# A two-block network on one core: the down factors kept as plain fp32 and split in the down stage, and all block sums on VectorE

## The chip, the core and the metric

The kernel runs on one core of one Trainium2 chip. The number that counts is the device time of one execution in microseconds (us). The engines of a core are named as the profile names them: PE is TensorE (PEld its weight loads), DVE is VectorE, ACT is ScalarE, POOL is GpSimd, and SP is SyncE, which here only issues DMAs. Every engine works through its own queue in the order in which the instructions stand in it; an instruction that has to wait holds up all that stand behind it on that engine.

## What is computed

Two transformer-like blocks run one after the other on 1024 tokens of width 1024. The change lies in their two feed-forward networks, which are alike in size (hidden width 2816):

```python
# first block
gu = jnp.einsum('bsd,df->bsf', x, w_gu)
gate, up = gu[..., :FFN_HIDDEN], gu[..., FFN_HIDDEN:]
ffn = jnp.einsum('bsf,fd->bsd', jax.nn.silu(gate) * up, w_down)
return layer_norm(DEEPNORM_ALPHA * x + ffn, ln2_g, ln2_b)
...
# second block
f = (jax.nn.silu(h @ w_gate[l]) * (h @ w_up[l])) @ w_down[l]
x = x + gate_f * rmsnorm(f, g_ffn_post[l])
```

All products are made in fp32 accuracy. The kernel splits each fp32 factor in a high part (a cast on ACT to the rounded type that PE takes) and a low part (the difference, on DVE or POOL) and makes three matmuls of them: high by high, high by low, low by high.

## The kernel before

**Stages.** The first feed-forward network (FFN1, tiles x1...) takes its gate and up products from about 751 us to 1226 us and its down stage until about 1405 us; the second (FFN2, tiles x3...) from about 2065 us to 2496 us and until about 2672 us. Before them, in between and after them lie the attention, mixing and output projections, which the change does not touch.

**Gate and up.** The hidden units go in pairs of blocks of 128. The first two pairs are made directly (`direct`), the other nine by a seven-product scheme for a 2x2 block matrix (class `Matrix`, Strassen-Winograd). A pair needs one `Gate` and one `Up` matrix of seven products each, a product being 12 matmuls of 128x512. For each product a weight factor is split into a tile `wst` (cast on ACT at L945; low part at L946, on POOL for products 2 and 4, else on DVE). Some weight factors are sums of blocks first (tile `tt`, L925, DVE). The results leave PSUM by DVE adds (tiles `u` and `p`, L963 to L976) and by ACT. The other factors of the seven products are blocks of the activations and sums of them: T1, T2, T3, T4, made once in `SAct.sums` (L838). Before, T1 and T4 are made on POOL, T2 and T3 on DVE; T4 is written into the tile of block B12 when the direct products have read that for the last time.

**The factors of the down stage.** The hidden activations of a pair are turned into seven left factors for the down products (`forms`, L1034: A11, A22, A12 and the sums S1 to S4, which write over a11, a12, a21 and s1 in place) and stored in DRAM (`store`, L1026). Before, `store` takes a slot "w", splits the factor in it (tile `hf`: cast on ACT, low part on DVE, L80 and L84) and stores both parts, 512 KB. A store is issued on ACT's queue only when the next one comes (`flush`). The slots "w" are six, and `wst` takes its tiles from the same six. In FFN1 a side task also runs through this stage: `cond_steps` multiplies rows of w_cond (`raw_c`, 512 KB a load) into `mod` on DVE.

**Down.** `down` (L1129) goes over the pairs in groups of 1, 2, 2, 2 and 2, with seven products in each. The left factors of a product lie in one of the seven tiles of the activations (`act.next`, a ring), to which DMAs bring both parts from DRAM. The right factors are blocks of w_down or sums of them (`st`), split into `ws` (ACT and DVE). PE goes through the products; each result is added to an accumulator by DVE (`dacc` and `acc`, L1196). After the groups `down_last` adds four hidden blocks that were kept as they are (`hl_d`).

**Order.** The program is recorded in source order, and a scheduler then sets each engine's order; work under `soon()` gets a high priority in it.

```python
SLOTS = {"raw": 3, "w": 6}
def slot(tag, shape, dtype, name):
    return strm.tile(shape, dtype, tag=tag, bufs=SLOTS[tag], name=name)
```

Of the kernel before, what the change touches and what calls it, by code (L numbers as in the profile page):

```python
# [9 lines left out]
F32 = mybir.dt.float32  # L10
F32R = mybir.dt.float32r
# [10 lines left out]
S = 1024  # L22
D = 1024
P = 128
# [14 lines left out]
def two_blocks(ctx: ExitStack, tc: tile.TileContext, a):  # L39
# [16 lines left out]
    def slot(tag, shape, dtype, name):  # L56
        return strm.tile(shape, dtype, tag=tag, bufs=SLOTS[tag], name=name)
# [16 lines left out]
    def soon():  # L74
        return tc.high_priority(offset=4000)
# [132 lines left out]
    for h, l, k0, nk in wu0:  # L208
        for j in range(nk):
            k = k0 + j  # L210
# [566 lines left out]
    class SAct:  # L777
# [4 lines left out]
        def __init__(self, name):  # L782
            self.name = name
            self.high, self.high_done = pool(f"{name}b")
            hi = [self.high.tile([P, 4, 512], F32R, name=f"{name}{n}")
                  for n in ("B11h", "B11l", "B21h", "B21l", "B12l", "B22h", "B22l")]
            self.t = {"B11": hi[0:2], "B21": hi[2:4], "B22": hi[5:7]}

            self.ring, self.n = hi, 0

        def second_half(self):

# [3 lines left out]
            self.t["T4"] = self.t["B12"]  # L796

        def next(self):
            self.n += 1
            return self.ring[(self.n - 1) % len(self.ring)]  # L800

        def __call__(self, n):
            if n not in self.t:
# [34 lines left out]
        def sums(self):  # L838
            def sub(n, ts, eng, x, y):

                t = self.temp()
                (xh, xl), (yh, yl) = ([b.bitcast(F32)[:, :, ts] for b in self(z)] for z in (x, y))
                eng.tensor_tensor(t, xh, yh, op=OP.subtract)
                eng.tensor_tensor(t, t, xl, op=OP.add)
                eng.tensor_tensor(t, t, yl, op=OP.subtract)
                self.part(n, ts, t, eng)
                return t

            chunks = [slice(c * P, (c + 1) * P) for c in range(4)]
            for ts in chunks:  # L850
                t1 = sub("T1", ts, G, "B12", "B11")
                sub("T3", ts, V, "B22", "B12")
                t = self.temp()
                xh, xl = (b.bitcast(F32)[:, :, ts] for b in self("B22"))
                V.tensor_tensor(t, xh, t1, op=OP.subtract)
                V.tensor_tensor(t, t, xl, op=OP.add)
                self.part("T2", ts, t, V)
            for ts in chunks:
                sub("T4", ts, G, "B21", "T2")

    def norm_stats(x):

# [37 lines left out]
    NLAST, SIZES = 4, (1, 2, 2, 2, 2)  # L900
    NPAIR = (NFT - NLAST) // 2
    FORMS = ("A11", "S3", "S2", "A22", "S1", "A12", "S4")
    h_d = [{n: dr.tile([P, 2, 512], F32, name=f"h_d{i}{n}") for n in FORMS} for i in range(NPAIR)]
    hl_d = [dr.tile([P, 2, S], F32, name=f"hl_d{i}") for i in range(NLAST)]

    class Matrix:

# [88 lines left out]
    class Ffn:  # L996
# [29 lines left out]
        def store(self, dst, x):  # L1026

            self.flush()
            t = slot("w", [P, 2, 512], F32R, "hf")
            with soon():  # L1030
                split(t[:, 0], t[:, 1], x)
            self.stores.append((dst, t.bitcast(F32)))

        def forms(self, i, b):  # L1034


            if i >= NPAIR:
                plain = lambda j, th: self.store(hl_d[2 * (i - NPAIR) + j][:, :, th * 512:(th + 1) * 512], b[j, th])
                for n in ((0, 0), None, (1, 1), (1, 0), None, (0, 1)):
                    if n:  # L1040
                        plain(*n)
                    yield
                return
            put = lambda n, x: self.store(h_d[i][n], x)
            put("A11", b[0, 0])
            yield
            yield
            put("A22", b[1, 1])
            yield
            put("A12", b[1, 0])  # L1050
            yield
            yield
            a11, a12, a21, a22 = b[0, 0], b[1, 0], b[0, 1], b[1, 1]
            s1 = self.post("s1")
            V.tensor_tensor(s1, a21, a22, op=OP.add)
            V.tensor_tensor(a21, a11, a21, op=OP.subtract)
            put("S3", a21)
            yield
            V.tensor_tensor(a11, s1, a11, op=OP.subtract)
            put("S2", a11)  # L1060
            yield
            put("S1", s1)
            yield
            V.tensor_tensor(a12, a12, a11, op=OP.subtract)
            put("S4", a12)
            yield
# [62 lines left out]
        def down(self, wd, res=None):  # L1129
# [24 lines left out]
            for g, np_ in enumerate(SIZES):  # L1154
# [18 lines left out]
                a = [ps_lg(), ps_lg()]  # L1173
                for m, (p, ln, rn) in enumerate(((1, "A11", "B11"), (7, "S3", "T3"), (6, "S2", "T2"), (4, "A22", "T4"),
                                                 (5, "S1", "T1"), (2, "A12", "B21"), (3, "S4", "B22"))):
                    hs, ws = act.next(), []
                    for j in range(np_):
                        DMA.dma_start(hs.bitcast(F32)[:, 2 * j:2 * j + 2, :], h_d[f + j][ln])
                        w = slot("w", [P, 2, 512], F32R, "ws")
                        with soon():  # L1180
                            split(w[:, 0], w[:, 1], block(rn, j))
                        ws.append(w)
                    if p in (7, 2):
                        b = [ps_mm(512), ps_mm(512), *(ps_tr().rearrange("p a b -> p (a b)") for _ in range(2))]
# [1 line left out]
                    for c0, n in ((0, 2), (2, 2)) if p in (1, 6, 5, 3) else ((c, 1) for c in range(4)):  # L1186
                        o = a[c0 // 2] if n == 2 else b[c0][:, None, :]
                        for i in range(n):
                            ts = slice((c0 + i) * P, (c0 + i + 1) * P)
                            for j in range(np_):  # L1190
                                mm3(o[:, i, :], hs[:, 2 * j, ts], hs[:, 2 * j + 1, ts], ws[j][:, 0], ws[j][:, 1],
                                    not more and j == 0, j == np_ - 1, more)
                        x = acc_of(p, c0, n)
                        with soon():
                            if g > 0:
                                V.tensor_tensor(x, x, o, op=OP.add)  # L1196
                            elif res is not None and p not in own:
                                V.scalar_tensor_tensor(x, x, ALPHA, o, op0=OP.mult, op1=OP.add)
                            else:
                                A.copy(x, o)  # L1200
                        q = {4: 6, 2: 1}.get(p)
                        if lastg and q:
                            V.tensor_tensor(x, x, acc_of(q, c0, n), op=OP.add)
                        elif lastg and p == 5:
                            x7 = acc_of(7, c0, n)
                            V.tensor_tensor(x7, x7, x, op=OP.add)
# [5 lines left out]
            halves = lambda t: [flat(t)[:, i * S:(i + 1) * S] for i in range(2)]  # L1212
            self.hs, self.ws = [], []
            for n in range(NLAST):
                t = act.next()
                DMA.dma_start(flat(t).bitcast(F32), hl_d[n].rearrange("p a b -> p (a b)"))
                self.hs.append(halves(t))
            for n in range(NLAST):
                t = halves(act.next()) if n else [slot("w", [P, S], F32R, "last") for _ in range(2)]
                split(*t, nxt[n])  # L1220
                self.ws.append(t)
            for done in (dp_done, self.pp_done, self.gp_done):
# [428 lines left out]
    n = 0  # L1651
# [121 lines left out]
```

## Time and profile before

| what | value |
|---|---|
| time, median of 3 runs (lowest, highest) | 2727.97 us (2725.17, 2728.15) |
| profiled execution: its time, its span | 2729.37 us, 2727.6 us |
| busy PE, DVE, ACT, POOL | 89%, 67%, 40%, 29% of the span |
| mean granted PE clock | 0.945 |
| feed-forward gate and up, FFN1 and FFN2 | 475 us and 431 us |
| down groups and last blocks' start, FFN1 and FFN2 | 179 us and 176 us |

The span runs from the first to the last instruction; 1.8 us of the execution lie around it. The four stages of the last two lines are 1261 us, 46% of the span. Busy shares over the whole span mix stages with different limits, so what a change does is read in its own stages: how many matmuls a stage holds, how long it takes, and what PE waited for in it.

### The profile page before, as it was taken

The numbers are of one execution on the slowest core, as the hardware profiler recorded it, in microseconds if no ns is written. First come the engines' busy times: TensorE is split into PE (matmuls) and PEld (weight loads), VectorE is DVE, ScalarE is ACT, GpSimd is POOL, SyncE is SP. The second block draws the span as 40 slices with busy tenths as digits, with TensorE's granted clock in tenths as the row PEclk, the third lists the DMA queues.
The fourth block names the chain that finished last, engine by engine and source line by source line (L and its number), as shares of the span: only waits on it lengthen the run. The fifth ranks groups of instructions, "written<-read, shape, count | busy, mean of one in ns | idle before, by whom it ended". The sixth has DMA issues, their size and how long they took to land.

```text
span 2727.6 us, 32854 instructions
## 1 busy us (share of the span) xinstructions
PE 2419.6 (89%) x11584; PEld 1977.9 (73%) x11584; DVE 1840.7 (67%) x3042; ACT 1099.3 (40%) x2013; POOL 784.8 (29%) x751
## 2 busy tenths in 40 slices
PE   8889997998988887889997989898888898999998
PEld 8868775886766665668876868677666666777886
DVE  4889789457667777758776366767555656556775
ACT  4559864243233222323226344445733323334221
POOL 2510235037422122120026042527552212122004
PEclk9999997999998998999998999999989999899999
DMA  4153546333435554567732434553414323337763
GB/s 175 59 153 113 147 137 178 83 98 105 162 127 190 178 179 158 179 249 252 261 141 108 129 105 132 175 159 100 164 58 151 139 108 125 114 124 254 252 226 124
DMA packets 171724, 414.00 MB, mean 152 GB/s; under 512 B 21788, under 2 KB 67868, under 8 KB 170536
## 3 DMA queue, kind: packets, MB, share of 16 engines
q1 hardware_dynamic: 149064, 337.45, 38.2%
q10 hardware_dynamic: 22496, 74.46, 6.8%
q8 instruction: 92, 1.51, 0.2%
q14 instruction: 72, 0.59, 0.1%
HBM read 278.65 MB, written 133.19 MB: 151 GB/s over the span
## 4 chain that ended last, share of the span: by engine, by line
PE 51%; DVE 10%; DMA 5%; POOL 4%; issue 3%; ACT 3%; SPq 0%; ACTq 0%; DVEq 0%; POOLq 0%
PE plg L97 8%; PE plg L98 7%; PE plg L99 7%; PE pmm L97 6%; PE pmm L98 5%; PE pmm L99 5%; PE ptr L99 2%; PE ptr L97 2%; PE ptr L98 2%; DMA raw_c<-in_w_cond_dram 1%; DVE hf L84 1%; DVE wst L946 1%; DVE tt L925 1%; PE plg L337 1%; DVE mod L1278 1%
## 5 line engine op out<-in xcount | busy, mean ns | idle before, releaser
L946 POOL TENSOR_TENSOR wst<-rw,wst 128x512 fp32r<-128x512 f32 x57 | 90.0, 1578 | 406.6 <-ACT wst L945 323.9
L84 POOL TENSOR_TENSOR wl<-raw,wh 128x1024 fp32r<-128x1024 f32 (+2 forms) x28 | 66.1, 2367 | 306.4 <-ACT wh L80 280.1
L337 PE MATMUL plg<-qk,qk 128*128 128x384 f32 (+4 forms) x480 | 127.3, 383 | 29.0 <-DVE mn L350 15.7
L946 DVE TENSOR_TENSOR wst<-tt,wst 128x512 fp32r<-128x512 f32 x144 | 118.5, 826 | 23.7 <-ACT wst L945 23.6
L945 ACT CAST wst<-tt 128x512 fp32r<-128x512 f32 x144 | 88.6, 618 | 73.4 <-PE plg L99 21.4
L1574 DVE TENSOR_TENSOR_SCAN sab<-sab 128x640 f32<-128x640 f32 (+7 forms) x64 | 99.9, 1566 | 20.7 <-ACT sab L1572 19.9
L278 ACT ACTIVATE junk_a<-xi,cand 128x1024 bf16<-128x1024 f32 (+1 forms) x124 | 109.0, 879 | 12.0 <-DVE cand L267 6.9
L337 PEld LDWEIGHTS plg<-qk,qk 128*128 128x128 f32 x480 | 83.7, 202 | 39.6 <-DVE mn L350 17.7
L1196 DVE TENSOR_TENSOR dacc<-dacc,plg 128x1024 f32<-128x1024 f32 x48 | 58.5, 1220 | 55.8 <-PE plg L99 55.8
L80 ACT CAST ws<-st 128x512 fp32r<-128x512 f32 x72 | 44.9, 628 | 127.2 <-PE plg L99 86.8
L162 PE MATMUL pmm<-wh,xh 128*128 128x256 f32 (+1 forms) x320 | 92.2, 289 | 1.7 <-DVE stgl L399 0.8
L163 PE MATMUL pmm<-wl,xh 128*128 128x256 f32 (+1 forms) x320 | 91.5, 286 | 0.0
L164 PE MATMUL pmm<-wh,xl 128*128 128x256 f32 (+1 forms) x320 | 91.4, 286 | 0.0
L351 ACT ACTIVATE e<-e,mn 128x128 f32<-128x128 f32 (+7 forms) x96 | 74.1, 773 | 35.5 <-DVE mn L350 34.5
L994 POOL TENSOR_TENSOR u<-u,u 128x512 f32<-128x512 f32 x36 | 48.2, 1338 | 139.3 <-DVE u L968 113.5
L80 ACT CAST wh<-raw 128x1024 fp32r<-128x1024 f32 x54 | 56.5, 1048 | 69.0 <-PE pmm L98 29.1
L97 PE MATMUL pmm<-xh,wh 128*128 128x512 f32 x192 | 79.2, 412 | 5.8 <-DVE oB L585 3.2
L692 PE MATMUL pmm<-woh,mixh 128*128 128x512 f32 x192 | 78.9, 411 | 5.1 <-ACT mixh L681 2.7
L98 PE MATMUL pmm<-xl,wh 128*128 128x512 f32 x192 | 77.3, 403 | 0.0
L99 PE MATMUL pmm<-xh,wl 128*128 128x512 f32 x192 | 77.2, 402 | 0.0
L693 PE MATMUL pmm<-wol,mixh 128*128 128x512 f32 x192 | 76.3, 397 | 0.0
L694 PE MATMUL pmm<-woh,mixl 128*128 128x512 f32 x192 | 75.8, 399 | 0.3 <-DVE mixl L84 0.3
(733 smaller groups left out, 8361.1 us busy)
## 6 DMA issues: line engine op xcount, KB each, us to landing
raw_c<-in_w_cond_dram SPq DMA_DIRECT2D x48, 512.0 KB, 4.7
qk<-qkd SPq DMA_DIRECT2D x72, 256.0 KB, 5.7
rw<-in_wgu_dram SPq DMA_DIRECT2D x36, 512.0 KB, 3.5
rw<-in_w_down_dram SPq DMA_DIRECT2D x26, 512.0 KB, 5.2
x_d<-acc SPq DMA_DIRECT2D x24, 512.0 KB, 2.6
qk<-qk2d SPq DMA_DIRECT2D x48, 256.0 KB, 4.6
raw<-in_wqk_dram SPq DMA_DIRECT2D x20, 512.0 KB, 4.1
raw<-in_w_down_dram SPq DMA_DIRECT2D x18, 512.0 KB, 5.2
```

The source lines that it names most:

```text
L80: A.copy(hi, src)
L84: eng.tensor_tensor(lo, src, hi.bitcast(F32), op=OP.subtract)
L97: T.matmul(out, lh, rh, start=start, stop=False, skip_group_check=more)
L98: T.matmul(out, lh, rl, start=False, stop=False, skip_group_check=more)
L99: T.matmul(out, ll, rh, start=False, stop=stop, skip_group_check=more)
L162: T.matmul(o, at(0, k, tb * P, P), h[:, j, :], start=(k == 0), stop=False)
L163: T.matmul(o, at(0, k, tb * P, P), l[:, j, :], start=False, stop=False)
L164: T.matmul(o, at(1, k, tb * P, P), h[:, j, :], start=False, stop=(k == KT - 1))
L278: A.activation(junk_a[:, :L], xi[self.blks[i]], AF.Sign, bias=c, accum_out=self.cnt[:, i:i + 1])
L337: T.matmul(pl[:, c, :n], q[:, isl], k2[:, c * n:(c + 1) * n], start=(j == 0), stop=last)
L946: (G if p in (2, 4) else V).tensor_tensor(wl, x, wh.bitcast(F32), op=OP.subtract)
L1574: V.tensor_tensor_scan(sa[:, ::-1], sa[:, ::-1], sa[:, ::-1], 1.0, op0=OP.mult, op1=OP.bypass)
```

## The change

The factors are stored as they are: `store` no longer splits and takes no slot, and `h_d` and `hl_d` are half as large. In the down stage a product's factors are loaded into a raw half tile (`next_raw`, four halves in the first two tiles of the ring) and split there into one of the other five tiles: the cast on ACT, the low part on POOL for products 1, 2, 4 and 3 and on DVE for 7, 6 and 5. The low part of product 3's `ws` goes from DVE to POOL. In `sums` T1 and T4 are made on DVE. The four last blocks are split in the same way (low part on POOL). In the changed file the lines behind L786 stand some lines lower: L945 is L952, L958 is L965, L983 is L990, L1023 is L1030, L1169 is L1173.

```diff
@@ -786,7 +786,7 @@
                   for n in ("B11h", "B11l", "B21h", "B21l", "B12l", "B22h", "B22l")]
             self.t = {"B11": hi[0:2], "B21": hi[2:4], "B22": hi[5:7]}
 
-            self.ring, self.n = hi, 0
+            self.ring, self.n, self.m = hi, 0, 0
 
         def second_half(self):
 
@@ -796,8 +796,15 @@
             self.t["T4"] = self.t["B12"]
 
         def next(self):
+
             self.n += 1
-            return self.ring[(self.n - 1) % len(self.ring)]
+            return self.ring[2 + (self.n - 1) % 5]
+
+        def next_raw(self):
+
+            self.m += 1
+            k = (self.m - 1) % 4
+            return self.ring[k // 2].bitcast(F32)[:, k % 2 * 2:k % 2 * 2 + 2, :]
 
         def __call__(self, n):
             if n not in self.t:
@@ -848,7 +855,7 @@
 
             chunks = [slice(c * P, (c + 1) * P) for c in range(4)]
             for ts in chunks:
-                t1 = sub("T1", ts, G, "B12", "B11")
+                t1 = sub("T1", ts, V, "B12", "B11")
                 sub("T3", ts, V, "B22", "B12")
                 t = self.temp()
                 xh, xl = (b.bitcast(F32)[:, :, ts] for b in self("B22"))
@@ -856,7 +863,7 @@
                 V.tensor_tensor(t, t, xl, op=OP.add)
                 self.part("T2", ts, t, V)
             for ts in chunks:
-                sub("T4", ts, G, "B21", "T2")
+                sub("T4", ts, V, "B21", "T2")
 
     def norm_stats(x):
 
@@ -900,8 +907,8 @@
     NLAST, SIZES = 4, (1, 2, 2, 2, 2)
     NPAIR = (NFT - NLAST) // 2
     FORMS = ("A11", "S3", "S2", "A22", "S1", "A12", "S4")
-    h_d = [{n: dr.tile([P, 2, 512], F32, name=f"h_d{i}{n}") for n in FORMS} for i in range(NPAIR)]
-    hl_d = [dr.tile([P, 2, S], F32, name=f"hl_d{i}") for i in range(NLAST)]
+    h_d = [{n: dr.tile([P, 512], F32, name=f"h_d{i}{n}") for n in FORMS} for i in range(NPAIR)]
+    hl_d = [dr.tile([P, S], F32, name=f"hl_d{i}") for i in range(NLAST)]
 
     class Matrix:
 
@@ -1026,16 +1033,13 @@
         def store(self, dst, x):
 
             self.flush()
-            t = slot("w", [P, 2, 512], F32R, "hf")
-            with soon():
-                split(t[:, 0], t[:, 1], x)
-            self.stores.append((dst, t.bitcast(F32)))
+            self.stores.append((dst, x))
 
         def forms(self, i, b):
 
 
             if i >= NPAIR:
-                plain = lambda j, th: self.store(hl_d[2 * (i - NPAIR) + j][:, :, th * 512:(th + 1) * 512], b[j, th])
+                plain = lambda j, th: self.store(hl_d[2 * (i - NPAIR) + j][:, th * 512:(th + 1) * 512], b[j, th])
                 for n in ((0, 0), None, (1, 1), (1, 0), None, (0, 1)):
                     if n:
                         plain(*n)
@@ -1173,12 +1177,18 @@
                 a = [ps_lg(), ps_lg()]
                 for m, (p, ln, rn) in enumerate(((1, "A11", "B11"), (7, "S3", "T3"), (6, "S2", "T2"), (4, "A22", "T4"),
                                                  (5, "S1", "T1"), (2, "A12", "B21"), (3, "S4", "B22"))):
-                    hs, ws = act.next(), []
+                    hr = act.next_raw()[:, :np_, :]
                     for j in range(np_):
-                        DMA.dma_start(hs.bitcast(F32)[:, 2 * j:2 * j + 2, :], h_d[f + j][ln])
+                        DMA.dma_start(hr[:, j, :], h_d[f + j][ln])
+                    hs = act.next()
+                    hh, hl = hs[:, 0:np_, :], hs[:, 2:2 + np_, :]
+                    ws = []
+                    with soon():
+                        split(hh, hl, hr, lo_eng="pool" if p in (1, 2, 4, 3) else "dve")
+                    for j in range(np_):
                         w = slot("w", [P, 2, 512], F32R, "ws")
                         with soon():
-                            split(w[:, 0], w[:, 1], block(rn, j))
+                            split(w[:, 0], w[:, 1], block(rn, j), lo_eng="pool" if p == 3 else "dve")
                         ws.append(w)
                     if p in (7, 2):
                         b = [ps_mm(512), ps_mm(512), *(ps_tr().rearrange("p a b -> p (a b)") for _ in range(2))]
@@ -1188,7 +1198,7 @@
                         for i in range(n):
                             ts = slice((c0 + i) * P, (c0 + i + 1) * P)
                             for j in range(np_):
-                                mm3(o[:, i, :], hs[:, 2 * j, ts], hs[:, 2 * j + 1, ts], ws[j][:, 0], ws[j][:, 1],
+                                mm3(o[:, i, :], hh[:, j, ts], hl[:, j, ts], ws[j][:, 0], ws[j][:, 1],
                                     not more and j == 0, j == np_ - 1, more)
                         x = acc_of(p, c0, n)
                         with soon():
@@ -1212,11 +1222,12 @@
             halves = lambda t: [flat(t)[:, i * S:(i + 1) * S] for i in range(2)]
             self.hs, self.ws = [], []
             for n in range(NLAST):
-                t = act.next()
-                DMA.dma_start(flat(t).bitcast(F32), hl_d[n].rearrange("p a b -> p (a b)"))
-                self.hs.append(halves(t))
+                r = flat(act.next_raw())
+                DMA.dma_start(r, hl_d[n])
+                self.hs.append(halves(act.next()))
+                split(*self.hs[n], r, lo_eng="pool")
             for n in range(NLAST):
-                t = halves(act.next()) if n else [slot("w", [P, S], F32R, "last") for _ in range(2)]
+                t = [slot("w", [P, S], F32R, "last") for _ in range(2)] if n < 2 else halves(act.ring[0] if n == 2 else act.next())
                 split(*t, nxt[n])
                 self.ws.append(t)
             for done in (dp_done, self.pp_done, self.gp_done):
```

How this moves instructions shows at two places. The first is ACT's queue in FFN2, at the turn of one pair to the next (the factors of pair 6 are being stored): `DMA h_d6...` are the stores, `hf` the split copies, `wst` the weight factors of the next products, `s11` and `p1` results that leave PSUM. Before:

```order
L1023 DMA h_d6A12_6161<-hf_18903 128x1024
L983 ACTIVATE s11_18943<-pmm_18884 128x512
L80 CAST hf_18949<-u2_18626 128x512
L945 CAST wst_18953<-tt_18954 128x512
L80 CAST hf_18974<-s11_18643 128x512
L945 CAST wst_18977<-tt_18908 128x512
L80 CAST hf_18995<-s1_18945 128x512
L945 CAST wst_18998<-rw_18882 128x512
L1023 DMA h_d6S3_6157<-hf_18949 128x1024
L1023 DMA h_d6S2_6158<-hf_18974 128x1024
L80 CAST hf_19017<-p1_18600 128x512
L1023 DMA h_d6S1_6160<-hf_18995 128x1024
```

The same place in the changed kernel:

```order
L1030 DMA h_d6A12_6161<-p1_18356 128x512
L990 ACTIVATE s11_18675<-pmm_18619 128x512
L952 CAST wst_18764<-rw_18759 128x512
L952 CAST wst_18782<-tt_18785 128x512
L952 CAST wst_18803<-rw_18759 128x512
L952 CAST wst_18820<-tt_18821 128x512
L965 COPY p1_18779<-pmm_18763 128x512
L1030 DMA h_d6S1_6160<-s1_18677 128x512
L952 CAST wst_18839<-tt_18783 128x512
L1030 DMA h_d6S3_6157<-u2_18379 128x512
L1030 DMA h_d6S2_6158<-s11_18396 128x512
L952 CAST wst_18857<-rw_18761 128x512
```

The casts `hf` are gone from between the casts `wst`, and the stores read the results themselves.

The second is POOL's queue in the down stage of FFN2: its whole work in the groups of two pairs before (`st` is a sum of blocks of w_down), from the last of gate and up on:

```order
L994 TENSOR_TENSOR u_19826<-u_19826,u_19964 128x512
L1169 TENSOR_TENSOR st<-rw 128x512
L1169 TENSOR_TENSOR st<-raw,rw 128x512
L1169 TENSOR_TENSOR st<-raw 128x512
L1169 TENSOR_TENSOR st<-rw 128x512 x2
L1169 TENSOR_TENSOR st<-raw 128x512
L1671 TENSOR_TENSOR fg<-acc,gpf 128x1024
```

A stretch of it in the changed kernel (`x3B11h` and `x3B11l` are the raw halves; `x3B12l` and its like get the split):

```order
L84 TENSOR_TENSOR x3B12l<-x3B11h,x3B12l 128x1024
L84 TENSOR_TENSOR ws<-raw,ws 128x512
L84 TENSOR_TENSOR x3B22l<-x3B11l,x3B22l 128x1024
L84 TENSOR_TENSOR ws<-rw,ws 128x512
L1173 TENSOR_TENSOR st<-raw 128x512
L84 TENSOR_TENSOR x3B12l<-x3B11h,x3B12l 128x1024
L1173 TENSOR_TENSOR st<-rw 128x512
L84 TENSOR_TENSOR x3B21h<-x3B11h,x3B21h 128x1024
L84 TENSOR_TENSOR x3B22l<-x3B11l,x3B22l 128x1024
L84 TENSOR_TENSOR x3B21l<-x3B11h,x3B21l 128x1024
```

A group there holds four low parts of 128x1024, two of `ws` and two sums on POOL, where it held two sums.

## Rows read from the trace of the kernel before

**Rows 1.** Windows: length, busy us (instructions) of PE, PEld, DVE, ACT, POOL, PEclk, DMA, GB/s.

```profile
751.00:1226.00 475.00, 393.98 (x1540) 300.47 (x1538) 335.42 (x438) 146.96 (x261) 108.10 (x70) 0.93 0.51 180
1226.00:1405.00 179.00, 177.87 (x756) 144.01 (x757) 141.26 (x187) 50.10 (x76) 11.08 (x7) 0.99 0.66 236
2065.00:2496.00 431.00, 380.05 (x1517) 292.25 (x1516) 262.09 (x366) 139.11 (x247) 93.82 (x69) 0.95 0.37 134
2496.00:2672.00 176.00, 175.27 (x757) 143.33 (x756) 130.12 (x172) 53.49 (x84) 8.60 (x6) 0.99 0.65 235
```

**Rows 2.** Windows of single groups of two pairs in the down stages (columns of rows 1).

```profile
1289.00:1328.00 39.00, 39.00 (x169) 31.60 (x168) 30.92 (x41) 8.69 (x14) 2.88 (x2) 1.00 0.68 241
1328.00:1366.00 38.00, 38.00 (x165) 30.77 (x164) 26.67 (x36) 7.96 (x13) 0.00 (x0) 1.00 0.67 245
...
2566.00:2605.00 39.00, 39.00 (x172) 31.99 (x171) 31.04 (x41) 9.18 (x16) 3.02 (x2) 1.00 0.68 244
```

**Rows 3.** PE's waits, FFN2, 2065 to 2496 us: releaser, us in total, times, longest.

```profile
PE pmm L97 <- ACT wst L945: 12.1, 7, 3.1
PE plg L97 <- ACT wst L945: 12.0, 7, 1.7
...
PE plg L99 <- DVE wst L946: 4.7, 7, 0.7
...
PE plg L97 <- ACT ws L80: 3.6, 1, 3.6
```

**Rows 4.** PE's waits, FFN1, 751 to 1226 us.

```profile
PE plg L97 <- ACT wst L945: 14.4, 5, 5.0
PE pmm L97 <- ACT wst L945: 13.5, 4, 6.6
PE plg L97 <- DVE u L966: 11.8, 7, 3.4
PE plg L97 <- DVE u L968: 11.4, 10, 3.7
...
PE plg L99 <- DVE wst L946: 8.2, 7, 1.8
```

**Rows 5.** Timeline of ACT, FFN2: start, length, operation, [idle before <- releaser].

```profile
2311.29 0.60 ACT L983 ACTIVATE s<-pmm 128x512 f32<-128x512 f32 x1 [6.93 <-PE pmm L99]
...
2321.75 0.62 ACT L945 CAST wst<-tt 128x512 fp32r<-128x512 f32 x1 [1.69 <-DMA h_d6S<-hf]
```

**Rows 6.** Timeline of PE, the same place.

```profile
2320.11 0.79 PE L97 MATMUL pmm<-x3B11h,wst 128*128 128x512 f32 x1 [3.14 <-ACT wst L945]
...
2321.13 0.63 PE L97 MATMUL plg<-x3T1h,wst 128*128 128x512 f32 x1
2321.55 0.63 PE L98 MATMUL plg<-x3T1l,wst 128*128 128x512 f32 x1
```

**Rows 7.** Timelines of POOL and DVE in the down stage of FFN1.

```profile
1316.86 1.29 POOL L1169 TENSOR_TENSOR st<-rw 128x512 f32<-128x512 f32 x1 [31.61 <-DMA rw<-in_w_down_dram]
...
1316.93 1.76 DVE L84 TENSOR_TENSOR ws<-raw,ws 128x512 fp32r<-128x512 f32 x1
1318.62 0.68 DVE L84 TENSOR_TENSOR ws<-rw,ws 128x512 fp32r<-128x512 f32 x1
```

**Rows 8.** Sizes: groups by line (busy us, mean ns); one DVE sum of the timeline.

```profile
L877 POOL TENSOR_TENSOR acc<-acc,ln1g 128x1024 f32<-128x1024 f32 x8 | 19.6, 2455 | 7.6 <-ACT acc L876 7.6
...
650.16 1.22 DVE L878 TENSOR_TENSOR acc<-acc,ln1b 128x1024 f32<-128x1024 f32 x1
```

**Rows 9.** Timelines around T4: POOL writes it, DVE waits.

```profile
753.76 5.87 POOL L817 TENSOR_TENSOR x1B12l<-tt,x1B12h 128x512 fp32r<-128x512 f32 x4 [37.83 <-ACT x1B12h L816]
...
755.09 1.74 DVE L925 TENSOR_TENSOR tt<-rw 128x512 f32<-128x512 f32 x1 [2.48 <-POOL x1B12l L817]
```

**Rows 10.** DMA issues in 2065 to 2496 us: count, KB each, median us to landing.

```profile
h_d4S<-hf ACTq DMA_DIRECT2D x4, 512.0 KB, 4.8
...
h_d3A<-hf ACTq DMA_DIRECT2D x3, 512.0 KB, 2.6
```

## The prediction

> **What bounds the kernel now.** I read the windows by stage first, then PE's waits in each stage, then the timelines at the places where PE waits. FFN2's gate and up hold 1517 matmuls and take 431 us [rows 1]. In a two-pair group of the down stage PE runs 172 matmuls in 39 us at full clock [rows 2], 0.227 us each; at that pace the 1517 are 344 us, so 87 us are lost. In FFN1 1540 matmuls are 350 us and take 475: 125 lost. The down stages lose next to nothing: 756 matmuls are 172 us of 179, and 757 are 172 of 176. So gate and up have something to give, and the down stages can only get worse, apart from their first wait.
>
> What ends the waits in gate and up is mostly `wst`, the weight factor of the next product: 12.1 + 12.0 + 4.7 = 28.8 us in FFN2 [rows 3] and 14.4 + 13.5 + 8.2 = 36.1 us in FFN1 [rows 4]. They come some seven times each, once a pair, at the turn to the next `Gate` matrix. ACT shows why: after its 6.93 us wait for the result `s11` it has four copies `hf` and four `wst` to cast in turn, and a `wst` waits for a slot "w" that a store (h_d6S) still holds [rows 5]. PE then waits 3.14 us, and the next matmuls start 0.43 us apart instead of 0.23 [rows 6]: after the wait the granted clock is at its lower level, 1.2 GHz, and the clock row of the stage says the same as a mean, 0.95 in FFN2 and 0.93 in FFN1 [rows 1]. That is 0.05 x 431 = 22 us and 0.07 x 475 = 33 us lost to the clock. DVE is 61% busy in FFN2's stage and 71% in FFN1's, and ACT about 32%: neither is a bound by its rate. It is the order of the queues and the six slots.
>
> **The change, part by part.**
>
> *Stores without a split.* Seven casts and seven subtractions of 128x512 a pair leave ACT and DVE, and no slot "w" is taken any more, so all six serve `wst`. In the new order of ACT the casts `wst` for the products behind `s11` follow one another with nothing but the stores between them, and stand further ahead. The 28.8 us of FFN2 can go whole and with them most of the clock's 22: at most 51 us. Something stays, since the casts still stand behind `s11`'s 6.93 us wait and DVE still makes `tt` and the bank additions in order. I take 0.85 of the waits and 0.8 of the clock's loss, and a few us of short idle around each wait: 24 + 17 + 4 = 45 us. In FFN1 two more causes remain that the change doesn't touch: PE waits 11.8 + 11.4 us for DVE's additions [rows 4], on a DVE that also works for `mod` and waits for `raw_c`. There I take 0.7 of the 36.1 us and 0.4 of the clock's 33: 25 + 13 = 38 us. The ends for both together are 0 and 51 + 69 = 120 us; 83 is nearer to the upper one since the row that names the slot [rows 5] repeats in each pair.
>
> *The first products of the down stage.* PE waits 3.6 us there for `ws` [rows 3], behind the last copies and stores `hf`. These go in both networks, 7.2 us. But the first left factors now need a load, a cast and a low part after it. Both factors of the first group are 128x512 and are loaded before the last products of gate and up end, so I count -5 us, between -7 and +7.
>
> *Splits in the down stage.* A two-pair group gets seven casts of 128x1024 on ACT, which is busy 8.7 of 39 us [rows 2] and takes them. DVE has 30.9 and 31.0 us of work in a full group and 26.7 in the lighter one of each network [rows 2]; about 30 on average. It loses two low parts of `ws` (0.68 each [rows 7]) and gets three of 128x1024 (1.22 each [rows 8]): 30 - 1.4 + 3.7 = 32.3 of 39 us. By its rate DVE keeps up. POOL gets four low parts of 128x1024 (2.45 us by the nearest row [rows 8]) and two of `ws` (1.3): with its two sums about 15 of 39 us.
>
> But the two get in each other's way: while POOL ran its sum of 1.29 us, the DVE subtraction that began 0.07 us after it took 1.76 us instead of 0.68 [rows 7], a loss of 1.08. DVE's additions out of PSUM are not held so; the two kinds alternate in DVE's queue. I take half of a POOL instruction as DVE's mean loss: 4 x 1.25 + 2 x 0.65 = 6.3 us, which makes 38.6 of 39 us. That is the edge; queue jitter will cost something, and I count +1 us a group, for eight groups +8 us. The lower end is 0. DMA is no issue here: half of the bytes of the factors go.
>
> The Trainium skill (SBUF — State Buffer, Who interferes with whom) speaks against this part: it says that a DVE instruction with two SBUF inputs and a POOL instruction that reads SBUF exclude each other for the whole instruction, whoever comes first. The trace agrees (the 1.08 us of [rows 7]). By this rule at its limit, with DVE always the one that waits, the sum would be that of the second rival below.
>
> *T1 and T4 on DVE.* 32 instructions of POOL in each network become DVE work of 0.68 us, 22 us a network. They lie under the direct products, which PE runs from tiles that are long ready; POOL's share of that stretch held DVE up by the same lock. The last four are the ones on the path: POOL needs 5.87 us for T4's low part, and DVE's first `tt` waits 2.48 us for it [rows 9]; four subtractions on DVE are 2.7 us. I count 0, between -4 and +4 a network.
>
> *Sum.* The profiled execution took 2729.4 us (span 2727.6 and 1.8 around it): 2729.4 - 45 - 38 - 5 + 8 = 2649 us. The median of the runs shown is 1.4 us below the profiled one, so I forecast **2648 us**.
>
> **The rivals.**
>
> *The next wait eats half.* With `wst` early, PE waits for DVE's additions to free the banks, as it does already for 11.8 + 11.4 us in FFN1 [rows 4], and keeps the low clock. Then 41 us are won instead of 83: 2690 us. For it: in FFN1 DVE stays near 60% busy with `raw_c` waits in its queue. Against: FFN2's waits on DVE's additions are short.
>
> *DVE becomes the bound of the down stage.* If DVE loses nearly all of every POOL instruction, 4 x 2.3 + 2 x 1.15 = 11.5 us, a group takes 32.3 + 11.5 = 43.8 us instead of 39: +4.8 x 8 = 38 instead of 8, which gives 2678 us. This decides when the mean loss a group is over 6.7 us. For it: the one row shows 84% of POOL's time lost. Against: half of DVE's work there reads PSUM.
>
> *The stores hold DVE (slower).* S2 and S4 are now written over s11 and p1 while the stores of A11 and A12 read them from there; before, the stores read the copies. DVE's subtraction for S4 must wait until A12 has landed, and behind it in DVE's queue stand a `wst`, a `tt` and the addition for T2's result. A store takes 2.6 to 4.8 us to land [rows 10] for 512 KB. If its issue came behind ACT's 6.93 us wait [rows 5], DVE would stand for up to 6.9 + 4.8 = 11.7 us a pair; today a pair's turn loses about 9 us (28.8 + 22 + short idle over seven). Then 16 turns cost 2.7 us more each, nothing is won, and with -5 and +8 the time is 2729 + 43 + 3 - 1 = 2774 us. It decides where the hold is over 9 us. Against it: in the new order A12's store stands ahead of `s11`, and it is half as large.
>
> *It doesn't show.* If the waits for `wst` came from `tt` and `s11` alone and not from the slots, the time would stay at 2729 +- 5 us.
>
> **How the numbers follow.** A difference of 0.2%, 5.5 us, is about what a measurement of this kernel can tell from none. Forecast 0.55; half eaten 0.15; DVE bound in down with the gain in gate and up 0.15; stores hold DVE 0.11; no effect 0.04. Faster 0.85, same 0.04, slower 0.11. The low end of the range is the upper end of the gain without its last part: 2729 - 120 - 7 = 2602; the high end takes half of the gain with the whole lock, 2690 + 30 = 2720, short of the slower case. Range 2602 to 2718.
>
> **What would show it.** Right: PE's waits for `wst` in FFN2 fall from 28.8 to under 6 us, the clock of the stage rises from 0.95 to 0.98 or more, the stage takes 386 us instead of 431 and FFN1's 437 instead of 475; in the down groups DVE is 36 to 39 of 39 us busy, with subtractions of over 1.5 us beside POOL's. Wrong: waits of PE for DVE's additions in gate and up that grow by more than 20 us in all; groups of over 41 us in the down stage; or DVE idle before its S4 subtraction for a store of A12.

## The result and the profile after

The kernel after takes 2555.7 us (median of 4 runs, 2548.4 to 2559.6), the kernel before 2728.1 beside it: a ratio of 0.9359, 95% interval 0.9329 to 0.9390. The forecast was 2648, in a range of 2602 to 2718. The direction was right, the size was not: 172 us went instead of 80.

The same four stages as in [rows 1], now of the kernel after (windows: length, then busy us and instructions of PE, PEld, DVE, ACT, POOL, then PE's clock, DMA share, GB/s):

```profile
747.00:1116.00 369.00, 356.75 (x1514) 282.41 (x1513) 295.68 (x371) 115.33 (x197) 109.76 (x64) 1.00 0.53 173
1116.00:1305.50 189.50, 184.09 (x781) 147.50 (x780) 173.91 (x190) 76.61 (x106) 83.47 (x41) 0.98 0.45 143
1962.00:2312.00 350.00, 347.94 (x1489) 278.71 (x1488) 212.54 (x298) 108.22 (x185) 98.46 (x64) 1.00 0.32 108
2312.00:2495.00 183.00, 179.94 (x782) 146.23 (x781) 168.90 (x175) 84.14 (x121) 84.74 (x41) 1.00 0.44 141
```

The four windows shrink from 1261 to 1091.5 us, which is 169.5 of the 172.5 us by which the span fell. Gate and up go from 475 to 369 us in FFN1 and from 431 to 350 in FFN2. The down windows look longer, but they hold 25 matmuls more than before each (and those of gate and up 26 and 28 fewer): the first down products now begin while the last ones of gate and up still run.

The length of a window less PE's busy time is what PE stood still. In FFN2 that was 431 - 380 = 51 us and is now 2; in FFN1 it was 81 and is now 12. PE's busy time over its matmuls shows what the clock gave back, if one takes all of it for the clock's: 0.2505 us each became 0.2337 in FFN2 (25 us over the stage), 0.2558 became 0.2356 in FFN1 (31 us), while the clock of the two rows rose from 0.95 and 0.93 to 1.00. PE's waits in FFN1's gate and up (747 to 1116 us: who was waited for, us in total, times, longest), against [rows 4]:

```profile
PE pmm L97 <- ACT wst L952: 2.4, 2, 1.6
PE plg L97 <- DVE u L973: 2.4, 2, 1.5
PE ptr L99 <- DVE wst L953: 2.3, 1, 2.3
PE pmm L99 <- DVE wst L953: 1.6, 1, 1.6
PE plg L97 <- DVE u L975: 1.2, 1, 1.2
```

and in FFN2's (1962 to 2312 us), all that is left of [rows 3]:

```profile
PE pmm L97 <- ACT wst L952: 1.7, 4, 0.5
PE plg L97 <- DVE p L978: 0.3, 1, 0.3
```

The waits for `wst` are 1.7 us in FFN2 and 7.0 in FFN1 (0.7 us of it in a row not shown), and the waits for DVE's additions `u`, 23.2 us in FFN1 before, are now 3.6. The forecast had left these as they were.

ACT shows why. Its waits in FFN2's gate and up before (2065 to 2496 us):

```profile
ACT s L983 <- PE pmm L99: 49.1, 8, 6.9
ACT hf L80 <- POOL u L994: 45.8, 11, 7.3
...
ACT wst L945 <- PE plg L99: 15.7, 9, 3.5
```

and after (1962 to 2312 us):

```profile
ACT wst L952 <- PE plg L99: 134.2, 57, 4.7
...
ACT s L990 <- PE pmm L99: 17.8, 8, 2.4
```

Before, ACT waited for results: for PE's `pmm` ahead of `s`, and for POOL's sums ahead of the casts `hf`. Now a cast `wst` waits 57 times for PE's last matmul with an earlier product, which sets a slot free. Most of the time ACT is as far ahead as the six slots let it be. Its timeline at a turn like that of [rows 5], here while pair 4 is stored (start, length, operation, [idle before <- releaser]):

```profile
2087.64 0.60 ACT L990 ACTIVATE s<-pmm 128x512 f32<-128x512 f32 x1 [2.41 <-PE pmm L99]
2088.14 0.61 ACT L952 CAST wst<-rw 128x512 fp32r<-128x512 f32 x1
...
2092.53 0.62 ACT L952 CAST wst<-rw 128x512 fp32r<-128x512 f32 x1 [2.13 <-PE plg L99]
```

The wait ahead of `s11` is 2.41 us and no longer 6.93. The forecast took the 6.93 us as given. They were an effect: with the slots taken again, in an experiment below, the longest of these waits is 7.3 us. That PE was late with `pmm` because it had waited for `wst` itself is my reading of it; no run shows that link alone.

### The profile page after: what moved, and what is told of

Same layout as the page of the kernel before. It is cut to its first block, busy times and chain, and to the rows that moved or that the text cites. A ratio compares the mean times of both kernels' runs of the same rounds, so it can differ in the third digit from the quotient of the medians.

```text
span 2555.1 us, 32817 instructions
## 1 busy us (share of the span) xinstructions
PE 2360.4 (92%) x11584; PEld 1950.4 (76%) x11584; DVE 1824.9 (71%) x2976; ACT 1089.5 (43%) x1949; POOL 850.5 (33%) x753
## 3 DMA queue, kind: packets, MB, share of 16 engines
q1 hardware_dynamic: 149064, 300.22, 37.8%
## 4 chain that ended last, share of the span: by engine, by line
PE 40%; DVE 7%; POOL 3%; ACT 2%; DMA 2%; issue 2%; SPq 0%; DVEq 0%; POOLq 0%; ACTq 0%
PE plg L97 5%; PE plg L98 5%; PE plg L99 5%; PE pmm L98 5%; PE pmm L97 5%; PE pmm L99 5%; PE ptr L98 1%; PE ptr L97 1%; PE ptr L99 1%; DVE ws L84 1%; PE plg L337 1%; DVE st L1173 1%; DVE acc L1206 1%; PE ptr L1607 1%; DVE sab L1585 1%
## 5 line engine op out<-in xcount | busy, mean ns | idle before, releaser
L953 POOL TENSOR_TENSOR wst<-rw,wst 128x512 fp32r<-128x512 f32 x57 | 96.0, 1686 | 495.2 <-ACT wst L952 205.7
L952 ACT CAST wst<-tt 128x512 fp32r<-128x512 f32 x144 | 89.2, 621 | 207.5 <-PE plg L99 125.4
L953 DVE TENSOR_TENSOR wst<-tt,wst 128x512 fp32r<-128x512 f32 x144 | 107.5, 749 | 21.3 <-ACT wst L952 20.5
L1585 DVE TENSOR_TENSOR_SCAN sab<-sab 128x640 f32<-128x640 f32 (+7 forms) x64 | 102.5, 1606 | 21.0 <-ACT sab L1583 20.3
L952 ACT CAST wst<-rw 128x512 fp32r<-128x512 f32 x86 | 53.2, 619 | 118.0 <-PE plg L99 74.9
L1001 POOL TENSOR_TENSOR u<-u,u 128x512 f32<-128x512 f32 x36 | 59.2, 1644 | 83.9 <-DVE u L983 61.8
L84 DVE TENSOR_TENSOR ws<-st,ws 128x512 fp32r<-128x512 f32 x72 | 77.8, 1097 | 2.5 <-ACT ws L80 2.4
```

The lines of the kernel that those rows point to most:

```text
L84: eng.tensor_tensor(lo, src, hi.bitcast(F32), op=OP.subtract)
L952: A.copy(wh, x)
L953: (G if p in (2, 4) else V).tensor_tensor(wl, x, wh.bitcast(F32), op=OP.subtract)
L1585: V.tensor_tensor_scan(sa[:, ::-1], sa[:, ::-1], sa[:, ::-1], 1.0, op0=OP.mult, op1=OP.bypass)
```

## The experiments

My theory was that the six shared slots "w" had been the cause. The first rival was the work of the splits in ACT's and DVE's queues; the sums of T1 and T4 and the bytes of the stores were others.

**The work alone.** The kernel after, with each split done again into tiles that nobody reads:

```diff
-            return self.pp.tile([P, 512], dtype, tag="post", bufs=12, name=nm)
+            return self.pp.tile([P, 512], dtype, tag="post", bufs=10, name=nm)
...
+            t = self.pp.tile([P, 512], F32R, tag="hf", bufs=2, name="hf")
+            with soon():
+                split(t, t, x)
             self.stores.append((dst, x))
```

> The kernel after, with the split at each store of gate and up done once more and thrown away, in two 2 KB tiles of its own (two of the twelve tiles of the sums are given up for them): ACT's casts and DVE's subtractions are back, the slots "w" and the store's bytes are not. Theory (the six shared slots were the cause): 2556 to 2590 us, PE's waits for wst under 15 us in each gate and up stage, clock 0.98 or more. Rival (the work in ACT's and DVE's queues was the cause): 2650 to 2720 us, waits for wst of 20 us and more in each stage, clock 0.95.

Measured: 2564.4 us (2561.0 to 2571.3). The work costs 9 us beside the 2555.7 (12 beside a later 2552.3 of the same kernel), nearly all in FFN1. PE's waits for `wst` are 1.6 us in FFN2 and 7.9 in FFN1.

**The slots alone.**

```diff
+            t = slot("w", [P, 2, 512], F32R, "hf")
+            with soon():
+                split(t[:, 0, :64], t[:, 1, :64], x[:, :64])
             self.stores.append((dst, x))
...
+            self.stores.append((held_d[self.held % 8], t.bitcast(F32)[:, :, :64]))
```

> The kernel after, where each store of gate and up also takes a slot "w" again, fills 64 of its 512 columns with a split and holds the slot until a 64 KB store of them has landed, behind the raw store in ACT's queue. The slots are taken as before, the work in the queues is about an eighth of it (plus fixed costs). Theory (slots): 2650 to 2720 us, waits for wst of 20 us and more in each gate and up stage. Rival (work): 2556 to 2600 us, waits for wst under 15 us.

Measured: 2693.9 us (2691.5 to 2695.4), 138 us over the kernel after. Gate and up of both (FFN1, FFN2), first with the work alone, then with the slots alone:

```profile
742.00:1122.00 380.00, 363.35 (x1515) 285.80 (x1514) 327.68 (x432) 149.20 (x258) 111.12 (x64) 0.99 0.50 168
1967.00:2318.00 351.00, 349.06 (x1492) 279.17 (x1491) 256.13 (x360) 141.90 (x246) 97.19 (x64) 1.00 0.30 108
```

```profile
742.00:1190.00 448.00, 388.85 (x1538) 298.64 (x1536) 309.78 (x440) 123.63 (x259) 98.85 (x67) 0.95 0.46 155
2026.00:2448.00 422.00, 376.95 (x1512) 290.95 (x1510) 240.33 (x366) 116.81 (x247) 90.80 (x68) 0.96 0.30 100
```

DVE and ACT are busier in the first pair, and the first pair is fast. The second has PE's lower clock again. And with the slots alone PE's waits for DVE's additions come back too (FFN1, 742 to 1188 us):

```profile
PE plg L97 <- DVE u L974: 17.3, 10, 3.4
PE plg L97 <- ACT wst L953: 12.6, 5, 5.6
PE plg L97 <- DVE u L976: 10.2, 10, 3.7
```

So the 23 us that I had called another cause come and go with the slots. Through which instructions isn't shown: in the kernel before, the longest of these additions (PE waits 3.7 us for it at 906 us) stands right behind a `mod` of the side task in DVE's queue, two others (985 and 1150 us) behind low parts `hf`, and the side task is in all of these kernels.

**Slots, work and bytes together.** As the last, with the whole split, and with both parts stored (512 KB) besides the raw store.

> The kernel after, where each store of gate and up also does the whole split into a slot "w" and stores both parts (512 KB) besides the raw store: slots, work and bytes are back, while the down stage and the sums stay as after. Theory (what gate and up gained came from the store's split and its slot): 2700 to 2750 us, the down stages as after (189 and 183 us). Rival (the sums on VectorE or another order of the queues gave a part of it): 2600 to 2680 us.

Measured: 2721.3 us (2713.3 to 2725.7), in the theory's range. Gate and up take 470 and 426 us again. The store's split, its slot and its bytes are thus worth 166 us (2721.3 - 2555.7). With the slots, the work and the bytes add 27 us; without them the work was 9 to 12.

**The kernel before, without the sharing.** All work and all bytes stay; only the slot is another:

```diff
-            return self.pp.tile([P, 512], dtype, tag="post", bufs=12, name=nm)
+            return self.pp.tile([P, 512], dtype, tag="post", bufs=10, name=nm)
...
-            t = slot("w", [P, 2, 512], F32R, "hf")
+            t = self.pp.tile([P, 2, 512], F32R, tag="hf", bufs=1, name="hf")
```

> The kernel before, with the split parts of the stores in one 4 KB tile of their own instead of the slots "w" (two of the twelve tiles of the sums are given up for it). All casts, subtractions, bytes and the sums on POOL are as before. Theory (slots): the waits for wst fall below 15 us in each gate and up stage and the time to 2570 to 2640 us. Rival 1 (the work in the queues): 2700 to 2730 us. Rival 2 (a single tile makes each cast hf in ACT's queue wait for the landing of the store ahead, and the casts wst stand behind it): over 2730 us.

Measured: 2588.0 us (2583.3 to 2593.3), a ratio of 0.9473 (0.9449 to 0.9497) to the kernel before (2733.6 beside it). A single tile (4 KB in each partition) that isn't shared gives 145 of the 172 us. PE's waits for `wst` fall to 2.4 us in FFN2; in FFN1 they are 20.3, over the 15 that I had named. What rival 2 said of ACT does happen: its casts `hf` wait 84 us for landings in FFN1's gate and up and 65 in FFN2's, by the sum of all their rows. It costs PE little, since the casts `wst` are far enough ahead and mostly wait for PE, as in the kernel after (ACT's waits, 751 to 1147 us, the first row of either kind):

```profile
ACT wst L945 <- PE plg L99: 62.9, 38, 4.6
...
ACT hf L80 <- DMA h_d4A<-hf: 8.0, 3, 6.0
```

A rival is left: the stores now have a tile besides the six slots, and no run gives the shared ring a seventh slot instead. How much of the 145 us is the room and how much the separation is not shown.

**Every second store in a slot.** Added to the slots alone, ahead of the slot's taking:

```diff
+            if self.held % 2:
+                return
```

> As slots_back, but only every second store of gate and up takes a slot "w" and holds it (and does its eighth of a split). Measured so far: 2556 us with no store in a slot, 2694 with every store. Theory (each take delays the casts wst that come after it): 2600 to 2650 us, between the two. Rival (the slots only hurt once the run of four stores behind s11 fills them): under 2585 us, since two of that run leave four slots free.

Measured: 2662.9 us (2660.8 to 2664.2). That is over both: half of the slots do 78% of the harm ((2663 - 2556) / (2694 - 2556)). The harm isn't proportional to the number of stores that take a slot, and two left free at the turn don't cure it.

**Slots without a store.** As the slots alone, without the small stores, so that nothing waits for a landing.

> As slots_back, but without the 64 KB stores: each store of gate and up takes a slot "w" and fills 64 columns with a split, and the slot comes free when VectorE's subtraction is done; nothing waits for a landing. Measured so far: 2694 us with the stores, 2556 us without the slots. Theory A (a slot is held until its store has landed, as the forecast put it): 2556 to 2610 us. Theory B (a slot is lost from its place in the ring on: it is handed out in the order of the program, and its cast stands in ACT's queue waiting for a sum that POOL or VectorE makes late): 2660 to 2695 us. Between the two, both count.

Measured: 2650.3 us (2644.3 to 2651.3). Of the 138 us that the slots cost, 44 go with the landings (and with the issues of the small stores in ACT's queue); 95 stay. That lies between the two theories, nearer to B: both count. ACT's waits in this kernel (FFN2, 2006 to 2406 us) show the larger part:

```profile
ACT s L991 <- PE pmm L99: 55.8, 9, 7.3
ACT hf L80 <- POOL u L1002: 38.6, 10, 5.6
...
ACT hf L80 <- POOL p L1002: 25.5, 8, 3.2
```

and so does its timeline:

```profile
2264.25 0.25 ACT L80 CAST hf<-u 128x64 fp32r<-128x64 f32 x1 [3.54 <-POOL u L1002]
...
2264.40 0.62 ACT L953 CAST wst<-raw 128x512 fp32r<-128x512 f32 x1
```

The slots are handed out in the order of the program. A cast `hf` that waits for a late sum of POOL keeps its place in the ring and in ACT's queue, and the cast `wst` behind it, which starts 0.15 us after it, has waited too. The landing that [rows 5] shows is the smaller part. How much of the 95 us is the queue's order and how much the ring's, no run here separates. Waits in ACT's queue alone are not enough, though: in the kernel before without the sharing ACT stands 87 and 92 us at casts `hf` in gate and up, here 99 and 87 (FFN1 and FFN2, all rows), and there it costs PE little. My reading is that without a ring in common the scheduler can set the casts `wst` ahead of them.

**The sums alone**, the kernel before with T1 and T4 on VectorE:

```diff
-                t1 = sub("T1", ts, G, "B12", "B11")
+                t1 = sub("T1", ts, V, "B12", "B11")
-                sub("T4", ts, G, "B21", "T2")
+                sub("T4", ts, V, "B21", "T2")
```

> The kernel before, with T1 and T4 alone moved to VectorE. Theory: the sums are no part of the gate and up gain; only the stretch of direct products shortens by some 6 us a network, so 2714 to 2728 us. Rival (VectorE work beside POOL's sums was held up by the lock and a large part of the waits of gate and up came from that): 2640 to 2700 us.

Measured: 2713.0 us (2707.2 to 2722.8), ratio 0.9930 (0.9906 to 0.9955): 12 to 26 us faster, close to the theory and short of the rival.

**The kernel after with the sums back on POOL** (the same edit the other way), beside the kernel after:

> The kernel after once more, unchanged, beside the two others of this group: 2548 to 2560 us. It is what the next two are compared with.

> The kernel after with T1 and T4 back on POOL, so that only the stores' part of the change is left. Theory (the sums shorten the direct products by some 6 us a network and the turn to gate and up a little, as they did alone in the kernel before): 2567 to 2580 us, the stretch of direct products 116 us and more instead of 110. Rival (with the slots free the sums no longer matter, as the forecast counted them): 2550 to 2562 us.

Measured: 2552.3 us (2551.4 to 2556.9) for the kernel after, 2576.5 (2570.5 to 2577.3) with the sums on POOL. They are worth 24 us. The stretches of direct products, from their first matmul to the scheme's first, shorten from 120.3 to 110.7 us in FFN1 and from 114.3 to 109.1 in FFN2, 15 of the 24; some 6 more lie in gate and up. PE's waits in FFN1's direct products, with the sums on POOL (634 to 752 us) and on VectorE (631 to 743 us):

```profile
PE ptr L833 <- DVE x1B12l L824: 8.4, 2, 4.6
PE plg L98 <- DVE x1B12l L824: 2.3, 1, 2.3
```

```profile
PE ptr L833 <- DVE x1B12l L824: 2.6, 2, 1.7
```

The forecast said that PE runs there from tiles that are long ready. It doesn't: its transposes `ptr` wait for DVE's low parts `x1B12l`, and DVE is held up by POOL. DVE in the kernel before, early in that stretch, and POOL at the same time:

```profile
657.55 0.67 DVE L817 TENSOR_TENSOR x1B22l<-ptr,x1B22h 128x512 fp32r<-128x512 f32 x1
658.15 1.47 DVE L843 TENSOR_TENSOR tt<-x1B22h,x1B12h 128x512 f32<-128x512 f32 x1
659.65 2.76 DVE L844 TENSOR_TENSOR tt<-tt,x1B22l 128x512 f32<-128x512 f32 x1
662.44 1.67 DVE L845 TENSOR_TENSOR tt<-tt,x1B12l 128x512 f32<-128x512 f32 x1
```

```profile
657.77 1.30 POOL L844 TENSOR_TENSOR tt<-tt,x1B12l 128x512 f32<-128x512 f32 x1 [0.76 <-DVE x1B12l L817]
659.02 2.84 POOL L877 TENSOR_TENSOR acc<-acc,ln1g 128x1024 f32<-128x1024 f32 x1
661.82 1.75 POOL L845 TENSOR_TENSOR tt<-tt,x1B11l 128x512 f32<-128x512 f32 x1
```

The three sums `tt` of T3 take 5.9 us where free ones of this size take 0.68 each; two of them run beside sums of T1, the one of 2.76 us beside a product of the layer norm (L877), which stays on POOL. The low part from PSUM ahead of them, beside POOL's L844, takes its 0.67.

**The lock in the down stage.** All low parts of a down group on VectorE, then all of the left factors on POOL:

```diff
-                        split(hh, hl, hr, lo_eng="pool" if p in (1, 2, 4, 3) else "dve")
+                        split(hh, hl, hr)
...
-                            split(w[:, 0], w[:, 1], block(rn, j), lo_eng="pool" if p == 3 else "dve")
+                            split(w[:, 0], w[:, 1], block(rn, j))
```

> The kernel after, with the four low parts of the left factors and the two of ws that POOL makes in a down group moved to VectorE. By the sizes, 30 - 1.4 + 3 x 1.22 = 32.3 us of VectorE's work a group become 32.3 + 4 x 1.22 + 2 x 0.68 = 38.5 of 39 us, without POOL's lock. If the lock takes half of POOL's time (the forecast's 38.6 us), nothing changes: 2550 to 2565 us. If it takes nearly all of it, this is faster, under 2545 us. If the lock takes little, VectorE is now the later one: over 2570 us.

```diff
-                        split(hh, hl, hr, lo_eng="pool" if p in (1, 2, 4, 3) else "dve")
+                        split(hh, hl, hr, lo_eng="pool")
```

> The kernel after, with the three low parts of the left factors that VectorE makes in a down group moved to POOL (seven of 128x1024 in all, about 17 us, besides two of ws). VectorE keeps 32.3 - 3.7 = 28.6 us of work. With half of POOL's time lost to the lock it needs 28.6 + 7 x 1.25 + 0.65 x 2 = 38.6 us, the same as after: 2550 to 2570 us. With nearly all of it lost it needs 28.6 + 7 x 2.3 + 2.3 = 47 us a group, 8 more for eight groups: 2600 to 2630 us. If POOL's low parts are hidden and the lock takes little: 2545 to 2556 us.

> The kernel after with all low parts of the down stage on VectorE, once more: 2551.7 us stood against 2555.7, closer than 0.2%. Theory (POOL's lock costs the down stage a few us in FFN1, where VectorE has most to do): 3 to 8 us under the kernel after of the same group. Rival (no difference): within 3 us of it.

Measured: 2551.7 us (2548.4 to 2552.4) and, in the group of the kernel after's 2552.3, 2552.1 us (2549.2 to 2555.7) with all on VectorE: no difference in the whole. With all on POOL 2564.0 us (2560.8 to 2569.9), 12 us more; 8 of them lie in FFN2's groups of two pairs (164.4 us instead of 156.7). That is the case of half of POOL's time. The lock is there all the same: DVE's subtractions for `ws` in FFN1's down stage (last columns: count, busy us, mean ns, idle before), in the kernel after and with all low parts on VectorE:

```profile
L84 DVE TENSOR_TENSOR ws<-st,ws 128x512 fp32r<-128x512 f32 x35 | 37.5, 1090 | 0.0
```

```profile
L84 DVE TENSOR_TENSOR ws<-st,ws 128x512 fp32r<-128x512 f32 x35 | 24.2, 694 | 0.0
```

What pays for the splits is DVE's idle time ahead of the additions of PE's results, in the kernel before (1226 to 1405 us) and after (1116 to 1306 us); with all low parts on VectorE it is 6.0 us:

```profile
L1196 DVE TENSOR_TENSOR dacc<-dacc,plg 128x1024 f32<-128x1024 f32 x24 | 29.3, 1220 | 27.5 <-PE plg L99 27.4
```

```profile
L1206 DVE TENSOR_TENSOR dacc<-dacc,plg 128x1024 f32<-128x1024 f32 x24 | 28.6, 1211 | 7.2 <-PE plg L99 7.2
```

The equal times of the two kernels hide a difference. The groups of two pairs (windows as in [rows 1]; FFN1, then FFN2), in the kernel before, after, and with all low parts on VectorE:

```profile
1248.40:1405.40 157.00, 157.00 (x674) 127.20 (x673) 123.30 (x160) 37.32 (x57) 8.48 (x6) 1.00 0.63 224
2517.80:2671.80 154.00, 154.00 (x674) 126.38 (x673) 118.37 (x157) 36.77 (x57) 5.64 (x4) 1.00 0.62 225
```

```profile
1143.10:1305.70 162.60, 158.59 (x674) 127.70 (x673) 152.93 (x161) 60.00 (x85) 67.37 (x32) 0.98 0.42 136
2338.60:2495.30 156.70, 154.87 (x674) 126.10 (x673) 151.21 (x154) 63.71 (x90) 71.01 (x32) 1.00 0.44 138
```

```profile
1138.30:1294.50 156.20, 155.13 (x673) 125.58 (x671) 149.13 (x180) 60.97 (x84) 18.15 (x9) 1.00 0.41 138
```

With all low parts on VectorE, FFN1's groups take 6 us less, but the last blocks behind them take 4 us more (59.1 instead of 54.8) and FFN2's 2 (4 in the run before that one). The 6 us are not the lock's alone: the kernel with the work alone has the same low parts on POOL, its subtractions for `ws` take 1181 ns, and its groups in FFN1 take 155.2 us. What the rows do show is that POOL's help saved DVE nothing: 152.93 us of DVE's time with it, 149.13 without.

## Why the prediction was wrong in size

*What bounds the kernel.* Right: the loss lay in gate and up, 87 and 125 us by PE's pace, and the shared slots were at its root. By the same pace 37 us of it are left.

*Stores without a split: the step that failed.* The forecast had the loss (212 us), then priced only what bore the name `wst` and a share of the clock, 120 us at most and 83 as its value. PE's standing still fell by 49 and 69 us where 28 and 25 were counted, and the clock gave 25 and 31 where 17 and 13 were. With all of the store's old work and slots back in the changed kernel, the term measures 166 us.

Two sentences of that step were false. "Two more causes remain that the change doesn't touch": the waits for DVE's additions went with the slots and came back with them (27.5 us). "The casts still stand behind s11's 6.93 us wait": that wait shrank to 2.41 us. Waits were left out, too: FFN2's for DVE's additions, called short, are 12.0 us in 13 times and went, and FFN1's 9.5 us for the factor `mh` of the side task are 1.0 after. And the mean clock put its whole loss at 22 and 33 us, where the time of a matmul (0.2505 and 0.2558 us against 0.227) gives 36 and 44. The range inherited it: its low end, 2602 us, was those 120 us and the first products' 7, and no more. (Its high end is 2720 by its own sum.) And the shares of 0.85, 0.8, 0.7 and 0.4 came from no row. When the waits are links of one circle, the name at its end prices one link only.

*The mechanism in [rows 5].* Half right. The forecast named the order of the queues and the slots that a store holds; a slot held until a landing is 44 us of the slots' 138, and the order in which ring and queue hand out the casts is the rest. That the order also holds up casts behind sums that POOL makes late, it didn't say.

*The first products of the down stage.* Right in sign: they now run among the last products of gate and up, and the 3.6 us wait for `ws` is gone. With the slots alone it is back (4.3 us), so it went with the slots as well.

*Splits in the down stage.* +8 us were forecast, and the eight groups of two pairs take 8 us more: 157.0 and 154.0 became 162.6 and 156.7. DVE's work was sized well, 38.2 and 37.8 us a group against 38.6. The time was in part luck: 5.6 of the 8 us lie in FFN1, where PE waits 3.7 us in two waits for an addition, and the kernel with the work alone shows that these aren't fixed by the splits. The Trainium skill (SBUF — State Buffer, Who interferes with whom) has it that a DVE instruction with two SBUF inputs and a POOL instruction that reads SBUF exclude each other, and the trace agrees with it: 1090 ns against 694 for the subtractions of `ws`. Its price in the whole time is none, as the runs with all low parts on VectorE show, since DVE has as much to do either way.

*T1 and T4.* Counted at 0 within 4 us a network; they are worth 24 us in all. The forecast said that the lock held DVE up in that stretch, but gave it no price, since it took PE's tiles there for long ready.

*The last blocks* were not costed. PE now waits for the factor `last`, 4.9 us in FFN1 and 3.4 in FFN2, and their matmuls take 54.8 and 50.4 us where the kernel before has 52.0 and 45.0, together 8 us more (2495 us to the end):

```profile
PE pmm L98 <- DVE last L84: 3.4, 1, 3.4
```

*The rivals.* None came true. No store stands among what DVE waits for in gate and up; the additions `u` didn't eat the gain but went with the cause; DVE is 92% busy in the down stage (173.91 of 189.5 us, 168.90 of 183), and PE waits for it only 5 us in FFN1 and 3 in FFN2. A store's hold shows on ACT alone: three copies `p1` wait 2.8 us each in FFN2.

Stage by stage, read between PE's matmuls (FFN1 and FFN2): the direct products went from 119.3 and 116.0 us to 111.3 and 110.1; the scheme's products up to the groups of two pairs from 496.8 and 452.5 to 396.1 and 376.6; then come the groups and the last blocks, as above. That is -14, -177, +8 and +8 us, 174 together, while the span fell by 172.5.

## What to carry over

Don't let a buffer that waits for late results come from the ring that feeds the next products: one tile of its own (4 KB a partition) was worth 145 us, without any work removed. When a stage's loss can be counted from its bound, begin with that number and ask which of the waits are links of one circle; a sum over the waits with one name is a lower end. A lock between two engines costs what lies on the path: most of the sums' 24 us came where PE waited for DVE's tiles, next to nothing where DVE had idle time. And before work is given to another engine, ask whether the lock takes back what it saves: in the down groups it did.

## What was not expected of the hardware

A DVE sum of 0.68 us took 2.76 us beside one 2.84 us instruction of POOL, and the three in a row 5.9 us instead of 2.0. PE's granted clock read 1.00 over the whole 350 us of FFN2's gate and up, where it stood still 2 us in all; with 51 us of waits, none longer than 3.6 us, the same stage had read 0.95.
